# Every operand of a product at a multiple of 256 bytes

## The chip, the core and the metric

The kernel runs on one core of a Trainium2 chip. Its time is the device time of one execution in microseconds (us). The engines are PE (matrix products; PEld are its weight loads), DVE (vector), ACT (scalar), POOL, and SP, which issues the DMAs. SBUF has 128 partitions; a tile takes a run of bytes at the same place in every partition. "Remainder" below is that place (the byte at which an operand begins in its partition) modulo 256.

## The reference

A batch of one sequence, S = 256 positions, width D = 1024, all in float32, goes through three blocks, each with a residual:

```python
h = x + ssd_mixer(rms_norm(x, norm_w[0]), ...)   # state-space mixer: in, conv, scan, gate, out
h = h + mla_mixer(rms_norm(h, norm_w[1]), ...)   # 16 heads with latent q and kv, rope, gate, out
h = rms_norm(h, final_norm_w)
...                                              # second part, one layer on h:
# u = rmsnorm(h, g_mix): block attention (8 heads, compressed and windowed keys), a 31-tap
# convolution with layer norm, two gates over 2 x 1024 columns, merge, out
# feed-forward: w_up (2 x 2816), 3-tap convolution, gelu gate, w_down; a gate with per-layer
# embeddings p_2; rmsnorm with g_final
```

## The kernel before, in words

**Products.** The activations stand transposed: channels on the partitions, the 256 positions along the free axis. So a projection is a chain of products with a 128x128 block of weights (stationary) and 256 columns of activations (moving). To keep float32 accuracy at the speed of float32r, `parts` (L288) makes of each activation tile a high half (`uh`, `gh`, `oh`, `mp`, `ch`, `fh`) and the rest (`ul`, `gl`, `ol`, `cl`, `fl`), and `split` (L191) makes of the weights `whi` (ACT, L182) and `wlo` (DVE, L188). `mm3` (L215) then issues three products for each block: `whi` with the high half, `wlo` with the high half, `whi` with the low half. Some weights stay whole (`raw`) and are multiplied in plain float32; such a product is two records of PE.

**Stages.** 0 to 34 us: the first norm and the first group; to 242: the state-space mixer (in-projection `w_si`, per group a scan with `pcb`, `pl`, `pe`, `py`; gates `pz`; out-projection with `gh`, `gl`); to 441: latent attention (`cqh`, `ckh`, `oh`, `ol`); to 636: block attention, convolution and merge (`no`, `ch`, `cl`, `mp`); to 826: feed-forward, in which 48 products of `w_up` with `uh`, `ul` alternate with 12 of `w_dn` with `fh`, `fl`; then the last gate and norm.

**Order.** `stream` (L195) loads 1 MB of weights at a time on SP's queue into `raw` (4 buffers) and splits them ahead of use (6 buffers each of `whi`, `wlo`). Tasks (softmax, norms, scans) are generators that `Flow` (L68) starts at due times in ns (`Y`, L47) between the products; the planner's costs depend on shapes and types only.

**Where tiles lie.** Pools are filled in the order in which tiles are first named, each tile rounded up to 32 bytes. The pool `const` begins 128 past a multiple of 256 and holds `vec` 2676 bytes (2688 rounded up), `cst` 4608, `n0` 32, `ones` 512, `maskb` and `identb` 256 each and `fg` 32, so that the weights that follow begin at remainder 64; the pool `acts` lies at the right end, which is 32 below a multiple of 256, and holds `uh` and `ul`, 8192 each. The small pool is not a multiple of 256 long either, and the first tiles of the attention stages (`fk`, `scq`, `nsq`, `ru`, ...) are 32 bytes each. The operands then begin at these remainders, in every one of their blocks:

| operand | remainder before |
|---|---|
| `raw`, `whi`, `wlo` | 64 |
| `uh`, `ul` | 224 |
| `x0` (first group), `gh`, `gl`, `fh`, `fl`, `ph`; `ag`, `sel`, `cumb` (scan) | 0 |
| `wdp` (weights of `pdt`) | 0 and 128 |
| `cqh`, `cql`, `ckh`, `ckl`, `oh`, `ol`, `knh`, `qnh` | 96 |
| `no`, `ch`, `cl`, `mp`, `kcmp`, `q` | 64 |
| `ones`, `maskb`, `identb` | 32 |

Of the kernel before, what the change touches and what calls it, by code (L numbers as in the profile page):

```python
# [8 lines left out]
FT = mybir.dt.float32  # L9
FR = mybir.dt.float32r  # L10
BF = mybir.dt.bfloat16
# [13 lines left out]
def columns(*parts):  # L25
    at, out = 0, {}
    for name, n in parts:
        out[name] = (at, n)
        at += n
    return out, at  # L30
# [6 lines left out]
    ("lnb", 4), ("bco", 8), ("gffn", 8), ("fcw", 132), ("fcb", 44), ("gple", 8), ("gfin", 8),  # L37
    ("posk", 16), ("posv", 16))

CST, NCST = columns(("ident", 128), ("tri", 128), ("strict", 128), ("cos", 256), ("sin", 256), ("swap", 128),  # L40
                    ("cmask", 128))
CMP, NCMP = columns(("cmpm", 64), ("diagk", 32), ("diagv", 128), ("fold", 32))

# [1 line left out]
EARLY = 384  # L45

Y = {'means': 2928, 'dt': 307, 'd0': 11250, 'ssd': 4915, 'xt': 1875, 'state': 2400, 'ssd_y': 294, 'gate_sum': 4500, 'gate_r': 10546, 'gate_next': 1200, 'r1': 15360, 'latent': 100, 'latent_r': 13500, 'rope': 400, 'scores': 167, 'softmax': 9000, 'pt': 2263, 'ru': 4320, 'conv': 6250, 'nsa_pt': 3000, 'nsa0': 100, 'nsa1': 1152, 'nsa2': 1562, 'cmp4': 800, 'blocks': 5000, 'cmp': 5857, 'cmp2': 1005, 'ln': 128, 'ln_sum': 236, 'ln_r': 6787, 'merge': 20240, 'norm': 2997, 'ffn': 13499}  # L47
WARM = (10, 6, 1, 6)
NATA = 1
NATB = 0  # L50
# [48 lines left out]
def build(tc, a, out):  # L99
# [4 lines left out]
    def open_pool(name, bufs=1, **kw):  # L104
        p = tc.tile_pool(name=name, bufs=bufs, **kw)
        pools.append(p)
        return p.__enter__()
# [4 lines left out]
    const = open_pool("const")  # L112
# [3 lines left out]
    acts = open_pool("acts", side="right")  # L116
    small = open_pool("small", bufs=3)
# [16 lines left out]
    def mx_ps(name):  # L134
        return bank(name, "mx")
# [17 lines left out]
    h = act.tile([128, 8, S], FT, name="h", bufs=1)  # L153
    vec = const.tile([128, NVEC], FT, name="vec")
    cst = const.tile([128, NCST], FT, name="cst")
    n0 = const.tile([128, 8], FT, name="n0")
    nc.sync.dma_start(n0, a["n0"])
    nc.sync.dma_start(h[:, 0:2], a["xT"][:, 0:2])
    ones = const.tile([128, 128], FT, name="ones")
    nc.gpsimd.memset(ones, 1.0)  # L160

    def V(name, i=0, n=1):
# [3 lines left out]
    def C(name):  # L166
        at, n = CST[name]
        return cst[:, at:at + n]

    ident, tri, strict = C("ident"), C("tri"), C("strict")  # L170
# [125 lines left out]
    class Residual:  # L296
# [27 lines left out]
        def means(self, out):  # L324

            yield Y["means"]
            p = mx_ps("st")
# [22 lines left out]
    pa = open_pool("ssm", bufs=2)  # L350
    uh = acts.tile([128, 8, S], FR, name="uh", bufs=1)
    ul = acts.tile([128, 8, S], FR, name="ul", bufs=1)
    x = (uh, ul)
    def warm(p, n):

        for _ in range(n):
            nc.tensor.matmul(p[:, :128], ones, ones, start=True, stop=True, skip_group_check=True)
# [9 lines left out]
    p = mm_ps("warm")  # L367
    warm(p, WARM[0])
    done(p)
# [4 lines left out]
    with tc.manual_schedule(engines={mybir.EngineType.DVE, mybir.EngineType.Activation, mybir.EngineType.PE}):  # L374
        pst = mx_ps("st")
        f0, x0, w0 = [], {}, {}
        ss = pa.tile([128, S], FT, name="ss", bufs=1)

        def square(k):
            s = ss if k == 0 else pa.tile([128, S], FT, name="sq0", bufs=2)  # L380
            nc.scalar.activation(s, h[:, k], AF.Square)
            if k:
                nc.vector.tensor_add(ss, ss, s)  # L383

        def first(k):
            for q in range(3 if k > 3 else 1):
                for i in range(4):
                    at = k % 2 * 512 + i * 128
                    o = outs[i][:, :S]
                    if k < 4:  # L390
                        mm(o, raws[k // 2][:, at:at + 128], f0[k], k == 0, False)
                    else:
                        mm(o, w0[k // 2][q == 2][:, at:at + 128], x0[k][q == 1], False, k == 7 and q == 2)

        def first_hi(k):
            x0[k] = [pa.tile([128, S], FR, name="x0", tag="y", bufs=18) for _ in range(2)]
            nc.scalar.activation(x0[k][0], h[:, k], AF.Copy, scale=n0[:, k:k + 1])

        def first_lo(k):
            nc.vector.scalar_tensor_tensor(x0[k][1], h[:, k], n0[:, k:k + 1], x0[k][0], op0=OP.mult, op1=OP.subtract)  # L400

        for k in range(4):
            u = pa.tile([128, S], FT, name="u0", tag="y", bufs=18)
            nc.vector.tensor_scalar(u, h[:, k], n0[:, k:k + 1], None, op0=OP.mult)
            f0.append(u)
            square(k)
        first(0)
        first(1)
        for k in range(4, 8):
            square(k)  # L410
        for k in range(4, 8):
            first_hi(k)
        col_sum(pst[:, :2], ss, True)
        first_lo(4)
        first_lo(5)
        m0 = small.tile([128, 2], FT, name="m0")
        r0 = small.tile([128, 2], FT, name="r0")
        mean_eps(m0, pst[:, :2], D)
        done(pst)
        rsqrt(m0, 2, r0)  # L420
        first(2)
        his = [split_hi(raws[i][:, :1024]) for i in (2, 3)]
        w0[2] = his[0], split_lo(raws[2][:, :1024], his[0])
        first_lo(6)
        first_lo(7)
        first(3)
        rb = mx_ps("rb")
        spread(rb, r0)
        nc.scalar.activation(r0b, rb[:, :S], AF.Copy)
        w0[3] = his[1], split_lo(raws[3][:, :1024], his[1])  # L430
        for k in range(8):
            u = pa.tile([128, S], FT, name="u", tag="y", bufs=18)
            nc.vector.scalar_tensor_tensor(u, h[:, k], n0[:, k:k + 1], rb[:, :S], op0=OP.mult, op1=OP.mult)
            us.append(u)
            parts(u, uh[:, k], ul[:, k])
            if k > 3:
                first(k)
        done(rb)
# [25 lines left out]
    def dt_task():  # L464
# [9 lines left out]
        done(p)  # L474
        yield Y["dt"]
        p = mx_ps("pdt")
# [24 lines left out]
        nc.vector.scalar_tensor_tensor(dt.rearrange("p b h -> p (b h)"), pp, 2.0, dtx, op0=OP.mult, op1=OP.add)  # L501
        for b in range(2):
            nc.vector.scalar_tensor_tensor(av[:, b], dt[:, b], -1.0, ea_h, op0=OP.mult, op1=OP.mult)
        av4 = pa.tile([128, 2, 4, 32], FT, name="av4", bufs=1)
        nc.vector.tensor_copy(av4, av[:, :, None, :].to_broadcast([128, 2, 4, 32]))
        ind = SS("ind")[:, None, :, None]
        nc.scalar.activation(cumb[64:], ind[64:].to_broadcast([64, 2, 4, 128]), AF.Copy)
        nc.scalar.activation(sel.rearrange("p i t -> p (i t)"), SS("sel"), AF.Copy)
        yield Y["d0"]

# [29 lines left out]
    def ssd(g, Bt, Ct, xt):  # L540
# [5 lines left out]
        while "d0" not in state:  # L546
            yield 1000
        yield Y["ssd"]

# [13 lines left out]
        done(p)  # L563
        yield Y["xt"]
        p = mx_ps("pxt")
# [26 lines left out]
        done(p)  # L592
        yield Y["state"]
        p = mx_ps("pst2")
# [119 lines left out]
    pm = open_pool("mla", bufs=2)  # L714
# [2 lines left out]
    r1 = small.tile([128, 2], FT, name="r1", bufs=1)  # L717
    r1b = pm.tile([128, S], FT, name="r1b", bufs=1)
    fkb = pm.tile([128, S], FT, name="fkb", bufs=1)
    fk = pm.tile([128, 2], FT, name="fk", bufs=1)  # L720
    scq = pm.tile([128, 2], FT, name="scq", bufs=1)
    nsq = pm.tile([128, 2], FT, name="nsq", bufs=1)
    maskb = const.tile([128, 128], BF, name="maskb")
    identb = const.tile([128, 128], BF, name="identb")
    nc.vector.tensor_copy(maskb, C("cmask"))
    nc.vector.tensor_copy(identb, ident)
    cqh = pm.tile([128, 3, S], FR, name="cqh", bufs=1)
# [275 lines left out]
    pn = open_pool("nsa", bufs=2)  # L1003
    pg = open_pool("nsa2", bufs=2)
    pc = open_pool("cmp", bufs=1)
    x = res.x
    state = {}
    ru = pn.tile([128, 2], FT, name="ru", bufs=1)
    ruh = pn.tile([128, 2], FT, name="ruh", bufs=1)
    scn = pn.tile([128, 2], FT, name="scn", bufs=1)  # L1010
    nsn = pn.tile([128, 2], FT, name="nsn", bufs=1)
    rub = pn.tile([128, S], FT, name="rub", bufs=1)
    r2b = pn.tile([128, S], FT, name="r2b", bufs=1)

# [64 lines left out]


    vsw = pn.tile([128, 2, S], FT, name="vsw", bufs=1)
    gts = pn.tile([128, 2, 24], FT, name="gts", bufs=1)
    def v_task2(pv):
        while "ru" not in state:
            yield 500
# [87 lines left out]
    def nsa_blocks():  # L1173
# [11 lines left out]
            transpose(pt[:, b * 128:(b + 1) * 128], sT[:, b * 128:(b + 1) * 128], ident)  # L1185

        sc = pg.tile([128, 2, 4, 32], FT, name="sc", bufs=1)
        mx = pg.tile([128, 16], FT, name="mxc", bufs=1)
        sm = pg.tile([128, 16], FT, name="smc", bufs=1)
        nc.vector.tensor_tensor(sc, pt[:, :S].rearrange("p (b j c) -> p b j c", b=2, j=4),  # L1190
                                CC("cmpm").rearrange("p (b c) -> p b c", b=2)[:, :, None, :].to_broadcast([128, 2, 4, 32]),
                                op=OP.add)
# [7 lines left out]
            nc.scalar.activation(sc[:, b], sc[:, b], AF.Exp, scale=scn[:, b:b + 1])  # L1200
        nc.vector.tensor_reduce(sm, sc3, axis=AX, op=OP.add)
        nc.vector.tensor_scalar(sm, sm, 1e-30, None, op0=OP.max)
        ri = pg.tile([128, 16], FT, name="ric", bufs=1)
        nc.vector.reciprocal(ri, sm)
        nc.vector.tensor_mul(ri.rearrange("p (b j g) -> p b j g", b=2, j=4),
                             ri.rearrange("p (b j g) -> p b j g", b=2, j=4),
# [210 lines left out]
        nc.scalar.activation(gab[i], zh, AF.Tanh)  # L1417


    lnh = pg.tile([128, 8], FT, name="lnh", bufs=1)  # L1420
    nc.vector.tensor_scalar(lnh, V("lng", 0, 8), 0.5, None, op0=OP.mult)
    chl = [None]

# [219 lines left out]
    p = mx_ps("st")  # L1643
    warm(wp, WARM[1])
    col_sum(p[:, :2], fin.ss[0], True, False)
    warm(wp, WARM[2])
    col_sum(p[:, :2], last[0], False)
    warm(wp, WARM[3])
    done(wp)
# [19 lines left out]
def pack(inp):  # L1669
# [54 lines left out]
    for c in ORDER + "zz":  # L1724
# [35 lines left out]
    i = np.arange(128)  # L1760
# [5 lines left out]
    c = {  # L1766
        "ident": np.eye(128), "tri": i[:, None] <= i[None, :], "strict": i[:, None] > i[None, :],
        "cos": np.cos(ang), "sin": np.where((i % 64 < 32)[:, None], -np.sin(ang), np.sin(ang)),
        "swap": (i[:, None] ^ 32) == i[None, :],
        "cmask": np.where(i[None, :] > i[:, None], NEG, 0.0), "cmpm": np.where(cm, 0.0, NEG),  # L1770
        "diagk": i[:, None] // 64 == j // 16, "diagv": i[:, None] // 16 == i // 64,
        "fold": i[:, None] % 32 == j,
# [24 lines left out]
```

## Time and profile before

| | us |
|---|---|
| median of 3 runs | 864.96 (863.14 to 865.23) |
| profiled execution, its own time | 863.92 |
| its span, first to last instruction | 862.0 |
| PE busy | 840.7 (98%) |
| DVE busy | 714.8 (83%) |
| ACT busy | 543.6 (63%) |
| DMA queues, share of 16 engines | 44% |

The granted PE clock is 0.994 of 2.4 GHz over the span. A product counts as busy from its issue until its last column has left, some 280 ns, while the next one starts after less than half of that: so "busy" says that PE is never without work, not that it works at its peak. The distance between two starts is what one product costs; it is read from the chain of waits, where undisturbed products of one kind are merged to a piece with its time and count.

### The profile page before, as it was taken

What the parts mean: (1) busy time and instruction counts of PE and PEld (TensorE: products, weight loads), DVE (VectorE), ACT (ScalarE), POOL (GpSimd) and SP (SyncE); (2) the same over time, 40 slices, a digit from 0 to 9 for tenths busy, and PEclk for the clock granted to TensorE, in tenths of its full rate; (3) what the DMA queues carried; (4) which work ended last, traced back from release to release, by engine and by line L of the source; (5) the groups of instructions that cost most, each with busy time, mean ns of one, the idle gap of its engine ahead of it and who ended that gap; (6) DMA issues with size and microseconds to landing.
All of it is one profiled execution on the core that took longest, in us unless ns stands there. A gap on an engine that the chain in (4) does not pass through costs nothing.

```text
span 862.0 us, 17387 instructions
## 1 busy us (share of the span) xinstructions
PE 840.7 (98%) x6886; PEld 806.6 (94%) x6886; DVE 714.8 (83%) x1549; ACT 543.6 (63%) x1113; POOL 53.8 (6%) x66
## 2 busy tenths in 40 slices
PE   8999999999999999999999998998999999999996
PEld 8888999999999999999999887887999999999996
DVE  6999999788758888886679998965879988988756
ACT  5765766555647688786636465974558666656543
POOL 0000000110210000000330000001020000000102
PEclk9999999999999999999999998999999999999999
DMA  8424434444525335154343852335442655645601
GB/s 339 157 98 160 183 118 177 160 169 162 196 96 206 122 103 185 53 193 168 126 163 117 308 211 75 123 144 198 148 159 102 244 200 190 216 167 187 213 2 50
DMA packets 21681, 137.68 MB, mean 160 GB/s; under 512 B 2528, under 2 KB 3552, under 8 KB 6752
## 3 DMA queue, kind: packets, MB, share of 16 engines
q1 hardware_dynamic: 21600, 136.58, 43.7%
q8 instruction: 54, 0.88, 0.4%
q14 instruction: 27, 0.22, 0.1%
HBM read 135.52 MB, written 1.05 MB: 158 GB/s over the span
## 4 chain that ended last, share of the span: by engine, by line
PE 86%; DVE 5%; ACT 5%; DMA 1%; issue 1%; POOL 1%; SPq 0%; POOLq 0%; DVEq 0%; ACTq 0%
PE pj L146 54%; PE acc L146 10%; PE pz L146 10%; PE po L146 3%; PE ps L146 2%; DVE cv L1129 1%; ACT whi L182 1%; DVE wlo L188 1%; PE pt L150 1%; PE py L146 1%; ACT rope_t L800 1%; PE s L146 1%; DMA h<-in_xT 1%; PE pc L146 1%; DMA raw<-in_w_si 1%
## 5 line engine op out<-in xcount | busy, mean ns | idle before, releaser
L188 DVE TENSOR_TENSOR wlo<-raw,whi 128x1024 fp32r<-128x1024 f32 (+3 forms) x243 | 287.0, 1186 | 48.8 <-ACT whi L182 46.3
L182 ACT ACTIVATE whi<-raw 128x1024 fp32r<-128x1024 f32 (+3 forms) x243 | 247.0, 1025 | 108.7 <-PE pj L146 65.3
L146 PE MATMUL pj<-uh,whi 128*128 128x256 f32 x896 | 256.2, 287 | 2.6 <-DVE zh L1046 2.6
L146 PE MATMUL pj<-uh,wlo 128*128 128x256 f32 x896 | 253.6, 283 | 1.3 <-DVE wlo L188 1.2
L146 PE MATMUL pj<-ul,whi 128*128 128x256 f32 x896 | 252.8, 282 | 0.0
L146 PEld LDWEIGHTS pj<-uh,whi 128*128 128x128 f32 x896 | 169.7, 190 | 5.8 <-DVE zh L1046 2.8
L146 PEld LDWEIGHTS pj<-uh,wlo 128*128 128x128 f32 x896 | 170.1, 190 | 2.6 <-DVE wlo L188 2.1
L146 PEld LDWEIGHTS pj<-ul,whi 128*128 128x128 f32 x896 | 169.9, 190 | 0.6 <-issue 0.4
L146 PE MATMUL pz<-uh,whi 128*128 128x256 f32 x256 | 73.9, 288 | 0.4 <-ACT v L864 0.4
L146 PE MATMUL pz<-ul,whi 128*128 128x256 f32 x256 | 71.9, 281 | 0.0
L146 PE MATMUL pz<-uh,wlo 128*128 128x256 f32 x256 | 71.8, 280 | 0.0
L321 POOL TENSOR_TENSOR ss<-sqh,ss 128x256 f32<-128x256 f32 x35 | 30.1, 871 | 431.2 <-ACT sqh L320 430.7
L1129 DVE SCALAR_TENSOR_TENSOR cv<-cc,vec,cv 128x252 f32<-128x252 f32 (+28 forms) x120 | 50.0, 457 | 0.0
L146 PEld LDWEIGHTS pz<-uh,whi 128*128 128x128 f32 x256 | 48.3, 189 | 0.6 <-ACT v L864 0.6
L146 PEld LDWEIGHTS pz<-uh,wlo 128*128 128x128 f32 x256 | 48.3, 189 | 0.0
L146 PEld LDWEIGHTS pz<-ul,whi 128*128 128x128 f32 x256 | 48.2, 188 | 0.1
L1556 DVE SCALAR_TENSOR_TENSOR vo<-v,vec,vo 128x255 f32<-128x255 f32 (+1 forms) x88 | 41.7, 478 | 0.9
L534 DVE SCALAR_TENSOR_TENSOR cacc<-pj,cwh,cacc 128x253 f32<-128x253 f32 (+2 forms) x84 | 38.8, 473 | 2.2 <-ACT cacc L532 2.2
L146 PE MATMUL pj<-u,raw 128*128 128x256 f32 x128 | 31.2, 382 | 1.0 <-DMA raw<-in_w_si 1.0
L1554 ACT ACTIVATE vo<-v,vec 128x256 f32<-128x256 f32 x44 | 25.7, 590 | 3.4 <-DVE v L1551 3.3
L146 PEld LDWEIGHTS pj<-u,raw 128*128 128x128 f32 x128 | 22.9, 190 | 4.4 <-DVE ss L383 1.3
L900 ACT ACTIVATE P<-ps,nb,scq 128x128 f32<-128x128 f32 (+1 forms) x32 | 15.9, 507 | 14.7 <-DVE nb L898 14.7
(470 smaller groups left out, 2015.1 us busy)
## 6 DMA issues: line engine op xcount, KB each, us to landing
raw<-in_w_si SPq DMA_DIRECT2D x22, 1024.0 KB, 4.7
raw<-in_w_up SPq DMA_DIRECT2D x22, 1024.0 KB, 4.7
raw<-in_w_in SPq DMA_DIRECT2D x16, 1024.0 KB, 4.6
raw<-in_w_so SPq DMA_DIRECT2D x8, 1024.0 KB, 4.6
raw<-in_w_mz SPq DMA_DIRECT2D x8, 1024.0 KB, 4.6
raw<-in_w_mo SPq DMA_DIRECT2D x8, 1024.0 KB, 4.6
raw<-in_w_dn SPq DMA_DIRECT2D x8, 1024.0 KB, 4.7
raw<-in_w_mkv SPq DMA_DIRECT2D x4, 1024.0 KB, 4.7
```

The source lines that it names most:

```text
L146: nc.tensor.matmul(o, l, r, start=start, stop=stop, skip_group_check=True)
L150: nc.tensor.transpose(o, i, ident)
L182: nc.scalar.activation(hi[:, :n], raw, AF.Copy)
L188: nc.vector.tensor_sub(lo[:, :n], raw, hi[:, :n])
L321: nc.gpsimd.tensor_tensor(ss, s, ss, op=OP.add)
L534: nc.vector.scalar_tensor_tensor(acc[:, j:], p[:, :S - j], cwh[:, (3 - j) * 32 + f:(3 - j) * 32 + f + 1], acc[:, j:], op0=OP.mult, op1=OP.add)
L800: nc.scalar.activation(t[i ^ 32:(i ^ 32) + 32], src[i:i + 32], AF.Copy)
L900: nc.scalar.activation(P[:, c0:c0 + n], s[:, c0:c0 + n], AF.Exp, bias=nb[:, b:b + 1], scale=scq[:, b:b + 1], accum_out=sm[:, b:b + 1])
L1129: nc.vector.scalar_tensor_tensor(o[:, j:], c[:, :S - j], V("c31", (30 - j) * 4 + i), o[:, j:], op0=OP.mult, op1=OP.add)
L1554: nc.scalar.activation(o, v, AF.Identity, bias=V("fcb", f), scale=V("fcw", 88 + f))
L1556: nc.vector.scalar_tensor_tensor(o[:, j:], v[:, :S - j], V("fcw", (2 - j) * 44 + f), o[:, j:], op0=OP.mult, op1=OP.add)
```

## The change

Nothing is computed differently, but for the constant `swap`, which no product used and which is no longer loaded. Tiles are placed otherwise:

- `ones`, `maskb`, `identb` are named right behind `cst`, before the 32-byte `n0`; `cst` is 512 bytes shorter; a pad of 192 bytes closes `const`. The sum is 16512 + 2688 + 4096 + 512 + 256 + 256 + 32 + 192 + 32 = 24576, where the weights begin (remainder 0).
- A pad of 480 bytes in `acts` moves `uh` and `ul` from 224 to 0.
- The small tiles of the stages (`fk`, `scq`, `nsq`, `ru`, `ruh`, `scn`, `nsn`, `gts`, `mxc`, `smc`, `ric`, `lnh`) go to the pool `small`, which becomes 2560 bytes long with its pad of 64 and with one buffer instead of three for `m0` and `r0`.
- `av4` takes a buffer of `sq0`.

All tiles named behind these then begin at multiples of 256: weights and all activations of the table at remainder 0.

```diff
-CST, NCST = columns(("ident", 128), ("tri", 128), ("strict", 128), ("cos", 256), ("sin", 256), ("swap", 128),
+CST, NCST = columns(("ident", 128), ("tri", 128), ("strict", 128), ("cos", 256), ("sin", 256),
                     ("cmask", 128))
+PAD = (48, 16, 120)
...
     cst = const.tile([128, NCST], FT, name="cst")
+    ones = const.tile([128, 128], FT, name="ones")
+    maskb = const.tile([128, 128], BF, name="maskb")
+    identb = const.tile([128, 128], BF, name="identb")
     n0 = const.tile([128, 8], FT, name="n0")
...
+    const.tile([128, PAD[0]], FT, name="pad", bufs=1)
+    small.tile([128, PAD[1]], FT, name="pad", bufs=1)
...
     ul = acts.tile([128, 8, S], FR, name="ul", bufs=1)
+    acts.tile([128, PAD[2]], FT, name="pad", bufs=1)
...
-        m0 = small.tile([128, 2], FT, name="m0")
-        r0 = small.tile([128, 2], FT, name="r0")
+        m0 = small.tile([128, 2], FT, name="m0", bufs=1)
+        r0 = small.tile([128, 2], FT, name="r0", bufs=1)
...
-        av4 = pa.tile([128, 2, 4, 32], FT, name="av4", bufs=1)
+        av4 = pa.tile([128, 2, 4, 32], FT, name="av4", tag="sq0", bufs=2)
...
-    fk = pm.tile([128, 2], FT, name="fk", bufs=1)
+    fk = small.tile([128, 2], FT, name="fk", bufs=1)
...
-    gts = pn.tile([128, 2, 24], FT, name="gts", bufs=1)
+    gts = small.tile([128, 2, 24], FT, name="gts", bufs=1)
```

## Rows read from the trace of the kernel before

**Rows 1.** The page, parts 1 and 4: busy time; the chain by engine.
```profile
PE 840.7 (98%) x6886; PEld 806.6 (94%) x6886; DVE 714.8 (83%) x1549; ACT 543.6 (63%) x1113; POOL 53.8 (6%) x66
...
PE 86%; DVE 5%; ACT 5%; DMA 1%; issue 1%; POOL 1%; SPq 0%; POOLq 0%; DVEq 0%; ACTq 0%
```

**Rows 2.** Stretch, length; busy us (instructions) of PE, PEld, DVE, ACT, POOL; clock; DMA.
```profile
92.00:138.00 46.00, 46.00 (x400) 44.60 (x400) 44.11 (x90) 31.99 (x61) 0.00 (x0) 1.00 0.37 129
462.00:546.00 84.00, 79.89 (x645) 71.40 (x644) 79.22 (x198) 50.91 (x117) 0.00 (x0) 0.96 0.48 179
664.00:790.00 126.00, 126.00 (x1083) 126.00 (x1082) 113.57 (x192) 78.23 (x119) 0.00 (x0) 1.00 0.55 198
```

**Rows 3.** Waits of PE (us, times, longest): whole span; 47 to 78 us.
```profile
PE pj L146 <- DVE zh L1046: 2.6, 1, 2.6
PE pcum L146 <- DVE av L505: 1.5, 1, 1.5
...
PE pj L146 <- DVE wlo L188: 0.6, 1, 0.6
```

**Rows 4.** Chain: start us, us, products; moving operands oh/ol, mp, uh/ul, uh/ul.
```profile
419.16 21.23 PE pj L146 x182
...
612.37 10.08 PE acc L146 x84
...
643.98 19.58 PE pj L146 x165
...
747.63 5.63 PE pj L146 x48
```

**Rows 5.** Chain, the same: moving operands gh/gl three times, then fh/fl.
```profile
194.29 6.81 PE acc L146 x60
...
213.03 7.07 PE acc L146 x60
...
220.10 21.20 PE pj L146 x180
...
796.39 29.69 PE pj L146 x262
```

**Rows 6.** By tile: duration in ns, least/median/most, first and last start.
```profile
L146 PE MATMUL pj<-fh,whi x88: 276/276/276, 796.2 to 825.8; 128*128 128x256 f32 x88
...
L146 PE MATMUL pj<-uh,whi x896: 277/281/583, 34.4 to 849.6; 128*128 128x256 f32 x180
...
L146 PE MATMUL pj<-mp,whi x64: 279/283/283, 622.3 to 635.4; 128*128 128x256 f32 x64
...
L146 PE MATMUL pdt<-uh,wdp x16: 277/280/468, 20.9 to 29.6; 128*32 128x256 f32 x16
...
L146 PE MATMUL pe<-ag,sel x16: 222/274/411, 51.7 to 147.9; 128*128 128x128 f32 x16
...
L146 PE MATMUL pl<-cumb,ag x16: 393/436/504, 50.9 to 147.6; 128*128 128x512 f32 x16
```

**Rows 7.** Groups by line (count | busy us, mean ns | idle); then the timeline.
```profile
L146 PE MATMUL pj<-ul,whi 128*128 128x256 f32 x896 | 252.8, 282 | 0.0
...
L146 PE MATMUL pz<-ul,whi 128*128 128x256 f32 x256 | 71.9, 281 | 0.0
...
L146 PE MATMUL pj<-no,raw 128*128 128x256 f32 x64 | 14.6, 380 | 0.0
...
587.69 0.81 PE L146 MATMUL pj<-no,raw 128*128 128x256 f32 x3
```

**Rows 8.** Groups by line of 47 to 78 and of 462 to 546 us.
```profile
L146 PE MATMUL pj<-ul,whi 128*128 128x256 f32 x38 | 10.7, 282 | 0.0
...
L146 PE MATMUL pj<-ul,whi 128*128 128x256 f32 x149 | 42.9, 289 | 0.0
```

**Rows 9.** Groups by line, whole span: two DVE instructions of one shape.
```profile
L1561 DVE TENSOR_TENSOR ge<-ge,vo 128x256 f32<-128x256 f32 x22 | 9.3, 423 | 1.7
...
L1046 DVE SCALAR_TENSOR_TENSOR zh<-pj,rub 128x256 f32<-128x256 f32 x16 | 6.7, 416 | 7.6 <-PE pj L146 4.1 <-ACT gab L1417 3.5
```

More of the change, by code (lines that the diff above doesn't have):

```diff
@@ L158, in build @@
     nc.sync.dma_start(h[:, 0:2], a["xT"][:, 0:2])
-    ones = const.tile([128, 128], FT, name="ones")
+    const.tile([128, PAD[0]], FT, name="pad", bufs=1)
+    small.tile([128, PAD[1]], FT, name="pad", bufs=1)
     nc.gpsimd.memset(ones, 1.0)
@@ L719, in build @@
     fkb = pm.tile([128, S], FT, name="fkb", bufs=1)
-    fk = pm.tile([128, 2], FT, name="fk", bufs=1)
[L721 to L724, printed above, removed]
+    fk = small.tile([128, 2], FT, name="fk", bufs=1)
+    scq = small.tile([128, 2], FT, name="scq", bufs=1)
+    nsq = small.tile([128, 2], FT, name="nsq", bufs=1)
     nc.vector.tensor_copy(maskb, C("cmask"))
@@ L1007, in build @@
     state = {}
[L1008 to L1011, printed above, removed]
+    ru = small.tile([128, 2], FT, name="ru", bufs=1)
+    ruh = small.tile([128, 2], FT, name="ruh", bufs=1)
+    scn = small.tile([128, 2], FT, name="scn", bufs=1)
+    nsn = small.tile([128, 2], FT, name="nsn", bufs=1)
     rub = pn.tile([128, S], FT, name="rub", bufs=1)
@@ L1187, in nsa_blocks @@
         sc = pg.tile([128, 2, 4, 32], FT, name="sc", bufs=1)
-        mx = pg.tile([128, 16], FT, name="mxc", bufs=1)
-        sm = pg.tile([128, 16], FT, name="smc", bufs=1)
+        mx = small.tile([128, 16], FT, name="mxc", bufs=1)
+        sm = small.tile([128, 16], FT, name="smc", bufs=1)
         nc.vector.tensor_tensor(sc, pt[:, :S].rearrange("p (b j c) -> p b j c", b=2, j=4),
@@ L1202, in nsa_blocks @@
         nc.vector.tensor_scalar(sm, sm, 1e-30, None, op0=OP.max)
-        ri = pg.tile([128, 16], FT, name="ric", bufs=1)
+        ri = small.tile([128, 16], FT, name="ric", bufs=1)
         nc.vector.reciprocal(ri, sm)
@@ L1417, in build @@
         nc.scalar.activation(gab[i], zh, AF.Tanh)
-    lnh = pg.tile([128, 8], FT, name="lnh", bufs=1)
+    lnh = small.tile([128, 8], FT, name="lnh", bufs=1)
     nc.vector.tensor_scalar(lnh, V("lng", 0, 8), 0.5, None, op0=OP.mult)
@@ L1768, in pack @@
         "cos": np.cos(ang), "sin": np.where((i % 64 < 32)[:, None], -np.sin(ang), np.sin(ang)),
-        "swap": (i[:, None] ^ 32) == i[None, :],
         "cmask": np.where(i[None, :] > i[:, None], NEG, 0.0), "cmpm": np.where(cm, 0.0, NEG),
```

## The prediction

> **What bounds the kernel now.** I read the page's busy shares first, then the chain of waits, then the busy time by stretch, then the waits of PE alone. The shares say that PE is in use 98% of the span and the chain that it is PE for 86% of it [rows 1]. The stretches show the next engine: DVE works 44.11 of 46 us in 92 to 138 us and 113.57 of 126 in the feed-forward stretch, 664 to 790, and PE has the full clock or nearly [rows 2]. The waits of PE are few, the longest 2.6 us [rows 3]. So the time is set by how closely PE sets one product after another, and the step to look at is the distance between two starts. A piece of the chain that holds one kind of product only gives it: its time divided by its count.
>
> Here the chain shows something that no wait explains. Nearly all work is one form, a float32r product with 128x128 weights and 256 moving columns; 256 columns at 2.4 GHz are 106.7 ns. Four undisturbed pieces whose moving operand does not begin at a multiple of 256 bytes take 19.58/165 = 118.7 ns a product (uh, ul, remainder 224), 5.63/48 = 117.3 (the same), 21.23/182 = 116.6 (oh, ol, remainder 96) and 10.08/84 = 120.0 (mp, remainder 64): 56.52 us for 479, 118.0 ns [rows 4]. Four pieces whose moving operand is at remainder 0 take 6.81/60 = 113.5 and 7.07/60 = 117.8 (gh, gl), 21.20/180 = 117.8 (gh, gl) and 29.69/262 = 113.3 (fh, fl): 115.2 on the mean [rows 5]. Weights are at remainder 64 in all of them. The gh pieces show that remainder 0 allows two rhythms; fh shows the better one unbroken over 262 products. The durations say the same: every fh product takes 276 ns, that is 106.7 and 169.3, while uh has 277 at least and 281 at the median and mp 283 [rows 6]. So a product loses up to 7 ns inside itself, and the loss goes with where its moving operand begins. In the feed-forward stretch both kinds alternate within microseconds, beside the same DVE, ACT and DMA work, so it isn't the stage.
>
> **The change, part by part.**
>
> Products at a new remainder. The same instructions remain; uh, ul go from 224 to 0, the weights from 64 to 0, oh, ol, the latent tiles and the attention tiles from 96, mp, ch, cl from 64. Of the 256-column form that are 3 x 896 and 3 x 256 with uh and ul [rows 7], and by the loops of the code 384 with oh and ol, 216 with the query latent, 192 with mp, 96 with ch and cl and 192 with the key latent on one side or the other: 4536 products. What they cost afterwards is not in the trace, since no 256-column float32r product there has both operands at 0. Bounds: the nearest rows are fh (weights at 64), 113.4 as the mean of the two good pieces, 36.50/322, and, for two operands with the same remainder, mp at 120.0. I take 113.4: fh, fl are like uh, ul after the change in that all moving tiles of a stretch have one place and the weights one, and the longest run of theirs keeps the good rhythm from end to end. That the weights matter less is shown by pdt: its weights lie at 0 and 128 already and are only 32 wide, yet with uh moving it takes 277 ns at least and 280 at the median like any uh product [rows 6]. A gain of 118.0 - 113.4 = 4.6 ns each.
>
> What of that reaches the end. In 47 to 78 and 462 to 546 us PE already waits for DVE's low halves of the weights and for zh [rows 3], and DVE is busy nearly throughout (79.22 of 84 us in the second [rows 2]); a faster product there only waits longer. These stretches hold 3 x 38 and 3 x 149 uh and ul products [rows 8], 561, and I count them at nothing. The other 3975 x 4.6 ns = 18.3 us. Of these I take off one in twenty, for products that stand just ahead of a wait or of a change of kind: 17.4 us. Next late is DVE in 92 to 138 us, whose 400 products [rows 2] could take at most 1.8 us from its 1.9 idle ones; in the feed-forward stretch a period of 48 uh products saves 0.19 of 7.0 us, so 126 us shrink to about 122.6 against 113.57 of DVE. Both still fit.
>
> Products in plain float32. Those with the tile `no` moving, at remainder 64, last 380 ns a record, and three of them in a row take 0.81 us [rows 7]: (810 - 380)/2 = 215 ns from start to start, 2 above the 213.3 of two times 256 columns. They lose next to nothing at remainder 64, so I count no gain.
>
> Other engines. DVE's zh, at remainder 64, takes 416 ns and ge, at 0, 423 for the same shape [rows 9]: the place does nothing for DVE, so I count no gain there, nor on ACT. The 7 ns between the two, over the 5% of the chain that is DVE [rows 1], some 100 instructions, are 0.7 us: the bound either way.
>
> The wider allocation. Tiles moved into the small pool keep one buffer each and were written once in their stage before; m0 and r0 lose buffers that nothing used; the pads are never written. av4 in sq0's buffer must wait for the products that read wdp, which end before dtT, and so before av, is made: nothing to wait for. What it would cost without that cover is the wait already there, 1.5 us of PE for av [rows 3]. Without the swap columns one load falls from 192 to 128 KB, beside a queue with time to spare. The moved addresses can let a tile at a stage border wait for another old tile than before: between 1.5 us less, if that wait of PE goes, and 2.6 more, its longest wait now [rows 3]; I take 0, as PE shows no wait at a border.
>
> The sum is 863.9 - 17.4 = 846.5 us against the profiled execution (span 862.0 and 1.9 around it); the median of the runs shown is 1.0 above that, so 848 us.
>
> The fh products need 6.6 ns beside their columns, no less, at remainder 0 [rows 5]. The Trainium skill, "TensorE: Matmul & The Clock Gate" (Back-to-back issue gap), has a gap of N/2.4 + 2.5 ns, 109.2 for 256 columns; by that the products would gain nearly twice as much, about what the third rival gives. By that rule no product would have lost anything to its place; the float32r rows here disagree.
>
> **The rivals.**
>
> Same remainder on both sides is the worst case. Where moving operand and weights share a remainder now, with mp (and ch, cl), products are slowest, 120.0, with 283 ns each at the median [rows 4, 6]; the 512-column pl products, both sides at 0, take at least 393 ns, 10 more than 213.3 and 169.3 [rows 6]. If what counts is the distance between the two readings and not the place itself, the change puts the whole kernel in that state: 4248 products lose 2.0 ns and the some 1000 at remainder 0 now (gh, fh, x0, ph) lose 4.8, together 13.3 us: 878. It decides from the first wide projection, 34 us on. Against it: pe, 128 columns and both sides at 0, has at its least the clean 222 ns = 53.3 and 169 [rows 6]. Chance 0.12.
>
> The better rhythm is not the one that comes. If the long stretches fall into gh's 117.8, uh gains 0.2 and fh loses 4.4: between 1 us less and 2 more, some 866. The same follows if the place isn't the cause at all. For it: gh held 117.8 over 180 products [rows 5]. Against it: fh. Chance 0.12. The Trainium skill, "SBUF — State Buffer" (Specifications), gives lines of 16 bytes, full bandwidth from two hits a line on and a price for each crossing; every tile here begins at a multiple of 32 and is read without gaps, so by that rule nothing would change. The trace disagrees: 113.3 and 117.3 ns stand side by side in one stretch.
>
> The weights' place costs too. If their remainder is what leaves 6.6 ns on fh, all 256-column products fall to about the 2 ns a record of plain float32 [rows 7], say 109: 3975 x 9.0 and 1000 x 6.2 ns, 42 us, and about 823. Nothing in the rows shows float32r so close. Chance 0.06.
>
> A mixture. Every break can leave PE in either rhythm, as it does with gh; on the mean of rows 5, 115.2, the gain is 2.8 ns, 10.6 us, and 854. Chance 0.14.
>
> **How the numbers follow.** Forecast 848 with 0.56, the mixture 0.14, no change 0.12, slower 0.12, the large gain 0.06. The forecast's own spread is 843 (561 products and gh's 240 gain as well, none taken off) to 851 (2.6 us of waits and 0.7 of other engines more); the range reaches over the mixture and no change, 838 to 868. Runs of this kernel can tell 0.3% from nothing, 862.4 to 867.6: faster 0.76, the same 0.11, slower 0.13.
>
> **What would show it.** In the chain, pieces of 48 uh products between the down-projections of 5.44 us where 5.63 stood, and a period of 6.8 us for 60 products where 7.0 stood; uh durations of 276 at minimum, median and nearly at maximum; mp at 276. DVE's own times unchanged, its share up. PE's waits for DVE a little longer in 47 to 78 and 462 to 546 us. I am wrong if uh stays at 280 or goes to 283 with 120 between starts, if the products speed up and the stage does not, or if fh itself becomes slower.

## The result, and the profile after

The changed kernel takes 875.05 us (median of 4 runs, 874.55 to 875.73) against 864.33 (863.14 to 865.23): 1.0125 times the time before, 95% interval 1.0108 to 1.0143. It is slower by 10.7 us, where 848 us were forecast. The profiled execution spans 872.7 us where 862.0 stood.

Busy time and the chain by engine, of the changed kernel [against rows 1]:

```profile
PE 850.7 (97%) x6886; PEld 817.0 (94%) x6886; DVE 715.2 (82%) x1549; ACT 544.0 (62%) x1113; POOL 53.9 (6%) x66
...
PE 91%; ACT 4%; DVE 3%; DMA 1%; POOL 0%; issue 0%; SPq 0%; DVEq 0%; ACTq 0%; POOLq 0%
```

PE has 10.0 us more of busy time with the same 6886 products; DVE, ACT and POOL have what they had. The granted PE clock is 0.998 over the span, where 0.994 stood. So it is neither a wait nor another engine nor the clock, but PE itself. The pieces of the chain (start us, length us, products) that answer to rows 4, with oh/ol, mp, uh/ul and uh/ul moving:

```profile
424.10 26.04 PE pj L147 x217
...
616.50 10.08 PE acc L147 x84
...
648.21 19.79 PE pj L147 x165
...
754.40 5.76 PE pj L147 x48
```

and those that answer to rows 5, with gh/gl three times and then fh/fl (the last piece holds 35 products of the next stage as well):

```profile
196.13 7.20 PE acc L147 x60
...
215.54 7.19 PE acc L147 x60
...
222.73 25.80 PE pj L147 x215
...
804.80 35.64 PE pj L147 x297
```

Divided by their counts, all eight give 119.8 to 120.0 ns. Before they stood between 113.3 and 120.0. The durations by tile (ns, least/median/most) say the same against rows 6:

```profile
L147 PE MATMUL pj<-fh,whi x88: 283/283/283, 804.6 to 836.0; 128*128 128x256 f32 x88
...
L147 PE MATMUL pj<-uh,whi x896: 277/283/470, 35.2 to 859.9; 128*128 128x256 f32 x180
...
L147 PE MATMUL pj<-mp,whi x64: 279/283/283, 626.4 to 639.5; 128*128 128x256 f32 x64
```

fh went from 276 to 283 in every single product, uh from 281 to 283 at the median, and mp stayed. Where the time came from is told by the steps: a step is the time from the start of one product to that of the next, taken here from consecutive records of one form (256 columns, 128x128 weights, 105 to 135 ns, so without waits): after, 5346 such steps take 119.82 ns on the mean. Before, sorted by the distance from the next weights' beginning to the moving operand's (modulo 256), 3252 at 160 (uh, ul) took 117.96, 995 at 192 (gh, fh and their like) 114.87, 660 at 32 (oh, ol, the latent tiles) 117.00, 330 at 0 (mp and its like) 119.58 and 83 at 224 118.34. The differences are 6.0 + 4.9 + 1.9 + 0.1 + 0.1 = 13.0 us. The span has grown by 10.7, so some 2.3 us did not reach the end. The chain shows it coming bit by bit: the piece that begins with gh starts 2.6 us later (220.10, now 222.73), the one with mp 4.1 (612.37, now 616.50), the one with fh 8.4 (796.39, now 804.80), and the end lies 10.7 later. From 220 to 612 us, where DVE sets the pace in part, only 1.5 us are added, though the same steps are 4.3 us longer there; up to 220 us the steps grow by 2.7 us and behind 612 by 6.2, as the chain does (2.6 and 6.6).

### The profile page after: what moved, and what is told of

Same layout as the page of the kernel before. It is cut to its first block, busy times and chain, and to the rows that moved or that the text cites. A ratio compares the mean times of both kernels' runs of the same rounds, so it can differ in the third digit from the quotient of the medians.

```text
span 872.7 us, 17390 instructions
## 1 busy us (share of the span) xinstructions
PE 850.7 (97%) x6886; PEld 817.0 (94%) x6886; DVE 715.2 (82%) x1549; ACT 544.0 (62%) x1113; POOL 53.9 (6%) x66
## 4 chain that ended last, share of the span: by engine, by line
PE 91%; ACT 4%; DVE 3%; DMA 1%; POOL 0%; issue 0%; SPq 0%; DVEq 0%; ACTq 0%; POOLq 0%
PE pj L147 57%; PE acc L147 10%; PE pz L147 10%; PE po L147 3%; PE ps L147 2%; PE pt L151 1%; ACT whi L188 1%; PE s L147 1%; PE py L147 1%; ACT rope_t L806 1%; DVE cv L1135 1%; DMA h<-in_xT 1%; PE pc L147 1%; DVE wlo L194 0%; PE st L147 0%
```

## The experiments

The theory: a product's time depends on the **distance** from the beginning of the weights to that of the moving operand, modulo 256 bytes. By it, distance 0 is slower than most of those that the kernel before had, and the change made every distance 0. The rivals: a place that is bad by itself (0 for the moving operand, or for the weights), the wider allocation, contention with DVE and ACT.

**map.** Products alone, nothing beside them; the loop in short:

```diff
+for m, w in PAIRS:          # bytes by which the operands are shifted
+    t = ps.tile([128, 512], FT, name="m" + label(m) + "_w" + label(w), tag="p", bufs=8)
+    for i in range(40):
+        k = i % 8
+        nc.tensor.matmul(t[:, :S], wm[:, w // 4 + k * 128:w // 4 + (k + 1) * 128],
+                         xm[:, m // 4 + k * S:m // 4 + (k + 1) * S], start=i == 0, stop=i == 39)
```

Expected:

> Leaves the whole computation out: 87 series of 40 float32r products (128x128 weights, 256 columns) with nothing beside them, the moving operand and the weights beginning at chosen bytes of their tiles. Distance theory: what counts is the distance between the two beginnings modulo 256; all series with both at the same remainder take 120 ns a product wherever they lie, moving 0 with weights 64 takes 113.4 (as fh did) or 117.8 (as gh did), 64 with 0 is another value than 0 with 64. Place theory (weights at 0 are slow by themselves): every series with weights at 0 takes 119 to 120 whatever the moving operand, and those with weights at 64 are spread as in the kernel before. If neither matters alone on an idle core (contention with DVE and ACT is the cause), all series take the same time, 109 to 113 ns.

The chain of this kernel. Letters count 32 bytes (a is 0, b 32, c 64, d 96, e 128, g 192, h 224, i 256, k 320, m 384, o 448, y 768): mk_wc is a moving operand at 320 with weights at 64.

```profile
182.94 4.79 PE mi_wa L43 x40
187.73 4.71 PE mi_wc L43 x40
192.44 4.75 PE mi_we L43 x40
197.19 4.71 PE mi_wg L43 x40
...
225.56 4.79 PE mk_wc L43 x40
...
268.22 4.79 PE mm_we L43 x40
...
310.85 4.79 PE mo_wg L43 x40
...
334.60 4.67 PE mb_wa L43 x40
...
344.00 4.79 PE md_wa L43 x40
...
434.00 4.80 PE my_wa L43 x40
```

Every series with equal remainders modulo 256 takes 4.79 or 4.80 us, 120 ns a product, wherever it lies. 64 of the series are an 8 by 8 table of multiples of 64 for both sides: its values repeat along the diagonals, 117.8 at distance 64 or 192 and 118.6 at 128. The place of one side does nothing by itself, and no other engine is needed. At the odd multiples of 32 there are four series each, of different places: 32 takes 116.7 to 116.9 ns, 224 118.2 to 118.4, and 96 119.7 to 119.9, so 0 is not the only slow distance. At 160 alone the four differ: 117.3, 118.6, 118.6 and 120.0. One thing was missed: 113.4 did not come at all, only 117.8.

**w64, w64m64, buh0.** The same question in the kernel: the weights alone 64 bytes further, both sides 64 bytes further, and the kernel before with uh and ul alone at 0.

```diff
 w64
-PAD = (48, 16, 120)
+PAD = (64, 0, 120)
...
-    small.tile([128, PAD[1]], FT, name="pad", bufs=1)
 w64m64
+PAD = (64, 16, 104)
 buh0 (to the kernel before)
     ul = acts.tile([128, 8, S], FR, name="ul", bufs=1)
+    acts.tile([128, 56], FT, name="pad", bufs=1)
```

> The changed kernel with the weights and raw tiles 64 bytes further on; all moving operands stay at 0. Distance theory: all products are then where fh was before (moving 0, weights 64); at 113.4 ns 4975 of 5536 products gain 120.0 - 113.4 = 6.6 ns, 33 us less than the changed kernel: 842 us; if the other rhythm of gh comes, 117.8, 11 us less: 864. Place-of-the-moving-operand theory (0 is bad there): no change, 875.

> The changed kernel with weights and moving operands all 64 bytes further on: both at 64, as mp was before. Distance theory: 120 ns as with both at 0, 875 us. Place theory (0 on either side is the slow place): products fall under 120, under 870 us.

> The kernel before with one pad: uh and ul alone move from remainder 224 to 0, weights stay at 64. Distance theory, and the forecast's own reason: they take fh's rhythm, 3456 products less the 561 that wait for DVE gain 118.0 - 113.4 = 4.6 ns, 13 us: 851 us. If moving operands at 0 are what slowed the changed kernel: 3456 products at 120, 867 to 870.

Measured: w64 853.72 us, 0.9884 of before (0.9868 to 0.9901); w64m64 876.43, 1.0145 (1.0130 to 1.0160); buh0 855.79, 0.9910 (0.9889 to 0.9931). 64 bytes on the weights turn 1.2% slower into 1.2% faster; the same 64 bytes on both sides give the loss back. That is the distance, and no place. Moving operands at 0 are good when the weights are at 64, so buh0 gains as the forecast's reason had it, with the weights left at 64. But both gains are smaller than expected, 853.7 for 842 and 855.8 for 851. The chain of w64, gh twice, then mostly ul and uh of the next projection, and in the feed-forward stage fh, uh and the tail:

```profile
192.62 6.80 PE acc L147 x60
...
211.35 7.07 PE acc L147 x60
218.42 25.32 PE pj L147 x215
...
756.00 1.36 PE acc L147 x12
757.36 5.44 PE pj L147 x48
...
784.56 33.66 PE pj L147 x297
```

113.3 (6.80/60, 5.44/48) and 117.8 (7.07/60, 25.32/215) stand side by side at one and the same distance, as with gh before [rows 5]. By consecutive starts 3744 of the 5209 steps at 192 are 115 ns or less and 1405 are 116 to 119; the mean is 114.63, not 113.4. All steps of w64 together are 640.6 - 612.5 = 28.1 us shorter than the changed kernel's, the time by 875.05 - 853.72 = 21.3. What became of the rest, in the busy times of w64, in the chain by engine, and the stretch 462 to 546 us (PE, PEld, DVE, ACT, POOL):

```profile
PE 824.6 (97%) x6886; PEld 789.4 (93%) x6886; DVE 713.1 (84%) x1549; ACT 543.6 (64%) x1113; POOL 53.5 (6%) x66
...
PE 76%; DVE 15%; ACT 6%; DMA 2%; issue 1%; POOL 1%; SPq 0%; POOLq 0%; DVEq 0%; ACTq 0%
```

```profile
462.00:546.00 84.00, 78.73 (x668) 68.55 (x667) 82.61 (x209) 53.28 (x127) 0.00 (x0) 1.00 0.55 201
```

PE's busy time falls by 26.1 us, its span by 22.4 (872.7 to 850.3): 3.7 us more of PE are idle, DVE holds 15% of the chain for 3% in the changed kernel, and has 82.61 of 84 us in the stretch that had 79.22 before [rows 2]. The share of the slower rhythm and DVE are what these figures show of the 12 us missing to 842.

**phase, phase2.** Does the moment of the start choose the rhythm? 8 series for each distance, each behind one product of another length; in short:

```diff
+for d in DIST:
+    for n in [192 + 6 * j for j in range(8)]:
+        mm(f, 7, 0, d, n, True, True)
+        for i in range(20):
+            mm(t, i % 8, 0, d, 256, i == 0, i == 19)
```

> Leaves the whole computation out: 16 distances from moving operand to weights (0, 16, ... 240 bytes), each with 8 series of 20 float32r products, and before each series one product of 192 to 234 columns, so that the series begin at different moments. One-rhythm theory (the distance alone sets the time): the 8 series of one distance agree within 1 ns, as all series of the first map did, 117.7 at 192. Two-rhythm theory (the distance sets which rhythms can hold, the moment of the start which of them comes): at 192 some series run at 113.3 and others at 117.8; at 0 all at 120.

> Leaves the whole computation out: as the second map, at 16 distances of which most lie between its steps (4, 8, 12, 16, 20, 24, 28, 32, 176, 184, 188, 192, 196, 200, 208, 248 bytes), 8 series of 20 products each. If the distance sets which rhythms can hold, 16 and 192 show 113.3 to 113.7 in part of their series again, and their neighbours change by steps, not smoothly; a distance at which all 8 series hold 113.3 would be the place to choose. If the good rhythm were chance alone, every distance shows it in some series.

The chain of phase, one series at distance 0 (da), then four consecutive ones at 192 (dg):

```profile
31.51 2.41 PE da L37 x20
...
271.46 2.30 PE dg L37 x20
...
273.85 2.38 PE dg L37 x20
...
276.32 2.31 PE dg L37 x20
...
278.72 2.37 PE dg L37 x20
```

By the starts behind the fourth product, the eight series at 192 hold 113.7, 113.4, 117.7, 113.7, 117.8, 113.5, 117.7, 113.7. In phase2 the same eight beginnings give the same order. So 192 has two rhythms; the length of the product ahead, and with it the moment of the start, chooses between them, and the one that comes then holds. At 0 seven series hold 119.2 or 119.3 and one 119.6; none is fast. At 96 all eight take 119.7 to 120.3, no less than at 0. At 160 the eight, all in one place, spread from 117.3 to 120.0, so the spread in the map was not the place. At 16 six of eight held 113.3 or 113.4 in phase and all eight 116.5 to 116.7 in phase2. Other series stood ahead there, and phase2 ran on another chip of the kind, so which of the two made the difference is not shown. Distances that are no multiple of 16 (4, 8, 20, 24, 188, 196, 200 and others) gave 117.7 to 123.3 on the mean of their eight series, 192 gave 115.1.

**uh192, w192.** The changed kernel with one part undone, and the distance with the other sign.

```diff
 uh192
-PAD = (48, 16, 120)
+PAD = (48, 16, 72)
 w192
+PAD = (32, 32, 120)
```

> The changed kernel with uh and ul alone moved by 192 bytes, weights and everything else at 0. Distance theory: 3366 uh and ul pairs go from 119.2 ns to the 114.6 that distance 192 has on the mean in the kernel with weights at 64; less the 561 that wait for DVE 2805 x 4.6 = 13 us: 862 us. If the loss of the change lies in the wider allocation or in the small products instead: 875.

> The changed kernel with the weights 64 bytes earlier, all moving operands at 0: distance 64 where weights at 64 had 192. If only the size of the distance counts, 64 to either side is the same: 853 to 854 us. If its sign counts too (the first map had 117.7 ns with durations of 279 at 64, and 117.8 with 281 at 192): 117.7 throughout, 119.2 - 117.7 = 1.5 ns on some 4980 products, 867 us.

Measured: uh192 862.86 us, 0.9985 of before (0.9975 to 0.9994), as the distance theory had it (its 3274 uh and ul steps at 192 take 114.95 ns, the 2071 others at 0 119.63); w192 864.57, 1.0003 (0.9994 to 1.0013). At distance 64 the mean step is 117.43 ns for the 114.63 at 192: the sign counts.

**own.** Which weights does a product collide with: its own, or those being loaded for the next?

```diff
+series("bothzero", [(0, 0)])              # (moving, weights) by turns
+series("ownzero", [(0, 0), (64, 64)])
+series("nextzero", [(0, 64), (64, 0)])
+series("none", [(0, 64)])
```

> Leaves the whole computation out: series of 40 products in which the distance of a product to its own weights differs from the distance of its moving operand to the weights of the product behind it. ownzero: own distance 0, to the next weights 192 and 64 by turns; nextzero: own 192 and 64, to the next weights 0; bothzero and none (192) as references; then 128 and 512 columns, 64-column weights, bfloat16 and plain float32, each at distance 0 and 192. If the load of the next weights, which runs beside the product, is what collides: nextzero 120, ownzero about 118. If a product's own two operands collide: the other way round. Both wide forms should lose once per weight load if the load is the cause (512 columns: the same few ns as 256, 213.3 + 6 to 13), in proportion to the columns otherwise; bfloat16 and plain float32 show no difference between 0 and 192.

Its chain; "zero" is distance 0 and "off" 192:

```profile
30.83 4.80 PE bothzero L44 x40
35.63 4.69 PE ownzero L44 x40
40.32 4.80 PE nextzero L44 x40
45.12 4.71 PE none L44 x40
...
102.00 4.42 PE narrowzero L44 x40
106.41 9.18 PE widezero L44 x40
115.59 4.54 PE halfzero L44 x40
120.13 4.38 PE bfzero L44 x40
124.52 8.64 PE plainzero L44 x40
133.15 4.41 PE narrowoff L44 x40
137.56 9.39 PE wideoff L44 x40
146.95 4.76 PE halfoff L44 x40
151.71 4.38 PE bfoff L44 x40
156.10 8.63 PE plainoff L44 x40
```

nextzero is as slow as bothzero (119.7 and 120.0 by starts) though no product has distance 0 to its own weights; ownzero takes 116.9. Three repeats agree. So the distance that counts is that of a moving operand to the weights of the next product. Their load runs beside it: in these series its record starts 2 to 5 ns after the product's and ends 189 to 196 ns after that start. That the two readings get in each other's way fits this; no run shows how. (The steps of nextzero are uneven, 116 to 130, with that mean.) bfloat16 takes 109.1 and plain float32 215.8 or 215.9 at either distance. Two expectations missed: with 512 columns 0 is the better one (9.18 us for 9.39), and so it is with weights of 64 columns (4.54 for 4.76), so "0 is slow" holds for the form of this kernel, not for float32r at large. By starts the wide products stand 14 and 20 ns over their columns, more than the 6 to 13 that one loss for each load would give, so this form does not bear out the load as the cause. Products of 128 columns take 110 ns at either distance, twice their 53.3 ns of columns. That the load of the weights bounds them is likely, but no narrow series with fewer weight columns was run to show it.

The Trainium skill, "SBUF — State Buffer" (A bandwidth-pool intuition that's wrong), gives TensorE a second, independent read port for weight loads. If that made the two readings independent in time, the place of the next weights would change nothing; nextzero against ownzero, 119.7 and 116.9 ns, disagrees for float32r. The Trainium skill, "TensorE: Matmul & The Clock Gate" (LDWEIGHTS), prices a load at its columns over 1.2, an estimate of 106.7 ns here, near the 110 of the narrow products; the load records, 188 to 192 ns with 128 columns and 134 with 64, give 0.84 to 0.91 ns a column for the 0.83 of that rule.

**w64u16, w64uh224.** Can the kernel with weights at 64 be bettered with uh at distance 16; and what does the wider allocation cost by itself?

```diff
 w64u16 (to w64)
+    def operand(name, n):
+        t = acts.tile([128, n], FR, name=name, bufs=1)
+        return t[:, 20:20 + 8 * S].rearrange("p (k s) -> p k s", k=8)
...
-    acts.tile([128, PAD[2]], FT, name="pad", bufs=1)
+    uh, ul = operand("uh", 2112), operand("ul", 2104)
 w64uh224 (to w64)
-PAD = (64, 0, 120)
+PAD = (64, 0, 64)
```

> The kernel with weights at 64, uh and ul alone moved from distance 192 to 16. If the 113.3 that six of eight series showed at 16 in the second map is what 16 brings: uh pairs go from 114.6 to 114.4 or less, 851 to 854 us. If 116.7, as in all eight series of the third map: 2805 x 2.1 = 6 us more, 860 us.

> The kernel with weights at 64, uh and ul alone back at 224: uh, ul, gh, fh then have the distances of the kernel before (160 and 192), and the wider allocation is kept; only oh, ol and mp, ch, cl differ (192 in place of 32 and 0: 675 x 2.4 and 300 x 5.2 ns, 3.2 us). Distance theory with an allocation that costs nothing: 864 - 3 = 861 us. If the allocation itself costs or saves time, it is off by that.

Measured: w64u16 861.98 us, 0.9980 (0.9970 to 0.9989), with 117.34 ns a uh step: the upper case, and w64 stays the best. w64uh224 861.95, 0.9974 (0.9963 to 0.9985): with before's distances on uh, ul, gh and fh and the new allocation it is within 1 us of the 861 worked out, so the allocation has no cost of its own that these runs show.

## Why the prediction was wrong

**The bound: right.** PE sets the time, by the distance between starts; the loss is all in PE's products and DVE's stage absorbed its part.

**The price of the 4536 products: wrong, and this is the step that failed.** The prediction took 113.4 ns for both sides at 0 from fh, and wrote "That the weights matter less is shown by pdt". It measured 119.8 to 120.0 in every undisturbed piece. In the rows that it used, weights lay at 64 throughout, so place and distance could not be told apart; fh was good because it lay 192 bytes from the weights (w64, w64m64). For the same reason the some 1000 products that had their moving operand at 0 already (gh, fh and their like) stood in the sum at nothing, though their weights moved from 64 to 0: they cost 4.9 us of the 13.0. pdt could not decide it. Its distances were 224 and 96 then, at which the map's series take 118.4 and 119.8 ns, beside 117.3 to 120.0 at uh's own 160: by distance, too, it could look like any uh product. Besides, its weights have 32 columns, and with 64 columns 0 was the better distance (own), so it is no row for the form in question. Now its distances are 0 and 128, and it goes from 280 to 283 at the median:

```profile
L147 PE MATMUL pdt<-uh,wdp x16: 277/283/470, 21.6 to 29.9; 128*32 128x256 f32 x16
```

The one row of the right form at distance 0, mp at 120.0 [rows 4], was on the page as the upper bound, and should have been taken.

**The rival that came: right in mechanism and price.** "The distance between the two readings and not the place itself" is what the runs show, and its 13.3 us of longer products are the 13.0 of the records. It forecast 878 for 875.05 because it let every product reach the end, where 2.3 us did not, and set out from a median 0.6 us higher. "The worst case" goes too far: 96 is as slow in the map. The evidence set against it was misread: pe, with 128 columns, was judged by its duration, while narrow products show no distance in own (4.42 and 4.41 us for 40). pl, named in its favour, was no support either, as 512 columns do better at 0.

**The better rhythm: half right.** gh's two rhythms are two states of one distance (phase); 113.3 is not owed to the place. That alone would have kept even the forecast's premise from its 848: buh0, which carries that premise out on uh and ul, gives 855.8. The prediction's own signs of being wrong came: uh at 283 with 120 between starts, and fh itself slower.

**What was right among the small terms.** Plain float32 with `no` moving is unchanged, and so is DVE at either place [rows 7, 9]; the wait for zh stays and that for av does not grow [rows 3]. One reading was wrong, without weight in the sum: without the swap columns a load falls from 384 to 320 KB, not from 192 to 128. The lines of the changed kernel for the first four:

```profile
L147 PE MATMUL pj<-no,raw 128*128 128x256 f32 x64 | 14.6, 380 | 0.0
...
L1567 DVE TENSOR_TENSOR ge<-ge,vo 128x256 f32<-128x256 f32 x22 | 9.3, 424 | 1.7
...
L1052 DVE SCALAR_TENSOR_TENSOR zh<-pj,rub 128x256 f32<-128x256 f32 x16 | 6.7, 418 | 5.6 <-ACT gab L1423 3.5 <-PE pj L147 1.9
```

```profile
PE pj L147 <- DVE zh L1052: 2.6, 1, 2.6
...
PE pcum L147 <- DVE av L513: 1.1, 1, 1.1
```

**Open.** That 192 and 64, one distance with two signs, differ, that 192 has two rhythms, and that one distance, 16 or 160, takes several times (117.3 to 120.0 at 160) was measured, not explained. Nothing tried forces the good rhythm.

## What to carry to other kernels

Rounding every operand to one boundary is not neutral: it gives a product's two operands the same remainder, and in this form (float32r, 128x128 weights, 256 columns) that costs 120 ns; no multiple of 32 in the map costs more. Stagger them: moving operands 192 bytes past the weights, modulo 256, had the shortest mean step of the distances that kernels of this case had (0, 16, 32, 64, 160, 192, 224). w64, the changed kernel with two pads altered, is 1.2% faster than the kernel before, and buh0, that kernel with one pad added, 0.9%. And when a row is to price a new state, ask whether it has that state in all that varies: rows with one side fixed can't tell a place from a distance.

## What the runs showed of the hardware that was not expected

- The period is 256 bytes: 0, 256, 512 and 768 on the moving side all take 120 ns with weights at 0.
- Distance 96 is as slow as 0 in the map (119.7 to 119.9 ns), while 64 and 128, on either side of it, take 117.7 to 118.6.
- With the operands at distance 192 a long row of products keeps 113.3 or 117.8 ns from its first products to the next break; in phase and phase2 the length of the product ahead decided which.
- The wide form is the opposite: 512 columns take 227.3 ns at distance 0 and 233.3 at 192 by starts, 14 and 20 over the 213.3 of their columns, where 256 columns at these two distances lose 7 to 13.
- Two bfloat16 operands at one remainder cost nothing: 109.1 ns at 0 and 109.2 at 192.
